# One exponential per unit of four heads over the compressed keys, rope tables on DVE, and a new issue order on every engine

## The chip, the cores and the metric

The kernel runs on one NeuronCore of a Trainium2 chip. The core has five instruction queues that run side by side and wait for one another only through semaphores: PE multiplies matrices (its weight loads are listed as PEld), ACT (ScalarE), DVE (VectorE) and POOL (GpSimd) work on tiles in SBUF and PSUM, and SP issues most DMAs. The metric is the device time of one execution in microseconds (us); less is better.

## What is computed

One decoder layer for 256 tokens of 1024 channels, all in float32. Cut to what matters here:

```python
h = rmsnorm(x, norm1_g); proj = h @ w_in                 # (256, 6308), split into the parts below
q_a = rope(rmsnorm(q_a)); k_s, k_w likewise              # 12 heads in 3 groups of 4, head width 64
kc = rope(rmsnorm(mlp(blocks of k_c))); vc = mlp(blocks of v_c)      # 15 compressed keys per group
s_cmp = q_a . kc * scale
p_cmp = softmax(where(c_end <= t, s_cmp, -1e30)) * mask  # 256 tokens x 15 keys, for each head
o_cmp = p_cmp @ vc
...                                                      # o_slc over chosen blocks, o_win over a window
y_a = gate0 * o_cmp + gate1 * o_slc + gate2 * o_win
y_b = dilated attention over (q_b, k_b, v_b)             # 12 heads in 3 groups
mixed = sigmoid(g_ma) * (y_a @ w_o_a) + sigmoid(g_mb) * (y_b @ w_o_b)
x = x + mixed @ w_out
out = x + square(relu(rmsnorm(x, norm2_g) @ w_up)) @ w_down
```

With 256 tokens all four selected blocks are always chosen, so the selected attention and the window attention are both plain causal attention here.

## The kernel before

**Products.** Every float32 matrix is split into two parts that PE multiplies fast: `hi` is a rounded copy and `lo` the rest, and a product is made of three matmuls (hi by hi, lo by hi, hi by lo). Weights come from HBM in 192 or so pieces of 128 x 768 (`raw`). For each piece ACT casts it to `wh` (line 345) and DVE subtracts to get `wl` (line 350); then PE uses it for 12 to 18 matmuls of 256 or 384 columns. The input x is scaled and split in the same way: ACT makes `hT0` (line 415), DVE makes `hT1` (line 416), from the four quarters `xg0` to `xg3` that SP loads.

**Stages.** First the projections for the compressed, selected and window keys and values, then the queries together with the small MLPs that make the compressed keys; then attention runs piece by piece between further projections (the dilated q, k, v and the gates); then the output projections, `w_out`, and the feed-forward layer, from about 275 us on, which is matmuls and weight splits and little else.

**A unit of attention** (`nsa(g, t)`) is one group of four heads and 128 tokens; there are six. For each head PE makes the scores in PSUM, DVE takes the negative maximum `nm` (line 791), and ACT computes `exp(score + nm)` into `P` for three segments: selected keys, window keys and the 16 columns of the compressed keys (line 781, `expo`). Each of these asks for the row sum (`accum_out`), for which ACT runs a second small instruction. DVE then takes reciprocals of the sums and multiplies them with the gates (lines 826 and 827), and `P` is scaled by them: on ACT for seven pairs of heads out of twelve (line 832), on DVE for four and on POOL for one (lines 836 and 838). PE transposes P, and ACT and DVE split it again (`phi`, `plo`).

**Rope tables.** Five tables `ropeg` (128 x 256) are the cosines and sines times a gain; POOL multiplies them in the opening (line 444).

**The order of the work.** Python generators write the program, and at the end `issue_order` fixes, for each engine, in which order its instructions stand: the table `ORDER` lists for each engine the numbers of the instructions as they were written. An engine takes its instructions strictly in that order. The residual input `x1` (1 MB) is loaded by SP at line 1101; the program's tiles share SBUF where their lives don't overlap, and a load into shared space has to wait for the last use of what was there.

Of the kernel before, what the change touches and what calls it, by code (L numbers as in the profile page):

```python
# [19 lines left out]
S = 256  # L20
# [14 lines left out]
     "vkb": 3, "vqb": 3, "pscale": "aaaaaavvavgv", "dbufs": 4, "cahead": 2, "oc": (), "seq": "gQKVqkvgggg", "vneed": "nsa5", "late": 999, "mbufs": 8, "mahead": 7, "cseg": "000000", "yact": "", "kvact": 0, "tab": "g", "b32": "v", "epsact": 0, "mlast": 1, "dchain": "dils0", "dneed": "nsa5", "dPb": 8, "dP": "P", "q2": 4, "l0": 8, "l1": 9, "l2": 7, "l3": 10, "hh": 3,  # L35
# [85 lines left out]
1 0 2 4 3 9+2 104 15 13 12 16 11 19 14 20 18 5 17 6 8 7 21+83 105+60 166 165 167+4 172 171 173+5 179 178  # L121
180+4 185 184 186+4 191 190 192+5 198 197 199+2""",
    "ACT": """
# [122 lines left out]
def hybrid_layer(ctx: ExitStack, tc: tile.TileContext, A, out):  # L246
# [802 lines left out]
    pump(proj(420, post_kv(2)))  # L1049
    od.add(make_rb())  # L1050
    st_["qa"] = [once([128, 6, S], F32R, f"qa{i}") for i in range(2)]
    st_["y"] = once([128, 8, S], F32, "y")

    def zipped(i):

# [231 lines left out]
```

## Time and profile before

| | |
|---|---|
| median of 3 runs | 459.05 us (459.05 to 459.7) |
| the profiled execution | 458.8 us |
| its span, from the first to the last instruction | 457.0 us |
| mean granted TensorE clock | 0.993 |

The profile is of one execution. The span leaves out 1.8 us that lie around it in the execution's own time. Where the text speaks of a clock, 1.0 is 2.4 GHz and 0.5 is 1.2 GHz. Times of instructions are counted from the start of the span.

### The profile page before, as it was taken

To read this page: it belongs to the slowest core of one execution; us is meant where nothing else is said; L and a number is where in the kernel's file an instruction comes from. 1 tells how busy PE (TensorE), PEld (TensorE's weight loads), DVE (VectorE), ACT (ScalarE), POOL (GpSimd) and SP (SyncE) were. 2 spreads that over 40 slices of the span, in tenths; PEclk is the share of its full clock that TensorE was granted. 3 is DMA by queue.
4 is the path that set the end of the run, shared out by engine and by line. 5 is a ranking of instruction groups with operands and counts; after the bars stand their busy time and mean duration, and the time that the engine had idled before them with its cause. 6 is when DMAs were issued, how large, how long until landed. Compare 5 with 4: busy or idle time off the path is not lost.

```text
span 457.0 us, 9071 instructions
## 1 busy us (share of the span) xinstructions
PE 445.6 (98%) x3413; PEld 431.1 (94%) x3413; DVE 358.0 (78%) x654; ACT 284.2 (62%) x622; POOL 83.7 (18%) x92
## 2 busy tenths in 40 slices
PE   4999999999999999999999999999999999999996
PEld 4999899899999999898999999999999999999996
DVE  3989999999999998899999886886856654555440
ACT  4855677678999778876775555665665634433330
POOL 2712121313041000200000001796322300000000
PEclk9799999999999999999999999999999999999999
DMA  8974586725535522541521647666666667677620
GB/s 304 367 244 146 154 287 181 236 89 167 157 105 141 171 70 71 175 140 68 162 82 42 199 128 231 201 193 186 205 184 195 183 187 210 185 216 199 179 78 13
DMA packets 29484, 76.92 MB, mean 168 GB/s; under 512 B 3664, under 2 KB 5120, under 8 KB 29312
## 3 DMA queue, kind: packets, MB, share of 16 engines
q1 hardware_dynamic: 28864, 74.77, 54.7%
q10 hardware_dynamic: 576, 1.57, 1.0%
q8 instruction: 27, 0.44, 0.4%
q14 instruction: 17, 0.14, 0.1%
HBM read 75.28 MB, written 1.05 MB: 167 GB/s over the span
## 4 chain that ended last, share of the span: by engine, by line
PE 93%; DVE 2%; ACT 2%; DMA 2%; issue 0%; ACTq 0%
PE acc L983 19%; PE acc L985 19%; PE acc L984 19%; PE acc L480 6%; PE acc L481 6%; PE acc L479 6%; PE tp L709 3%; PE acc L468 2%; DMA raw<-in_kv_c 2%; PE sp L754 1%; PE pvo L721 1%; ACT wh L345 1%; PE pvo L723 1%; PE tp L552 1%; PE dsp L920 1%; PE hacc L615 1%
## 5 line engine op out<-in xcount | busy, mean ns | idle before, releaser
L350 DVE TENSOR_TENSOR wl<-raw,wh 128x768 fp32r<-128x768 f32 (+2 forms) x183 | 177.6, 979 | 61.7 <-ACT wh L345 57.2
L345 ACT CAST wh<-raw 128x768 fp32r<-128x768 f32 (+1 forms) x182 | 149.6, 833 | 102.1 <-PE acc L984 74.5
L983 PE MATMUL acc<-u,wh 128*128 128x256 f32 x256 | 71.6, 280 | 0.0
L984 PE MATMUL acc<-u,wh 128*128 128x256 f32 x256 | 71.6, 280 | 0.0
L985 PE MATMUL acc<-u,wl 128*128 128x256 f32 x256 | 71.5, 279 | 0.0
L984 PE MATMUL acc<-h,wh 128*128 128x256 f32 x256 | 69.0, 280 | 0.0
L983 PE MATMUL acc<-h,wh 128*128 128x256 f32 x256 | 69.0, 279 | 0.0
L985 PE MATMUL acc<-h,wl 128*128 128x256 f32 x256 | 66.1, 279 | 0.0
L480 PE MATMUL acc<-wl,hT 128*128 128x384 f32 (+1 forms) x164 | 55.1, 350 | 0.3 <-DVE wl L350 0.3
L479 PE MATMUL acc<-wh,hT 128*128 128x384 f32 (+1 forms) x164 | 54.7, 348 | 0.0
L481 PE MATMUL acc<-wh,hT 128*128 128x384 f32 (+1 forms) x164 | 54.6, 347 | 0.0
L1159 POOL TENSOR_TENSOR r<-r 128x256 f32<-128x256 f32 x32 | 27.7, 866 | 128.7 <-ACT r L1158 127.5
L985 PEld LDWEIGHTS acc<-u,wl 128*128 128x128 f32 x256 | 48.2, 188 | 0.0
L983 PEld LDWEIGHTS acc<-u,wh 128*128 128x128 f32 x256 | 48.1, 188 | 0.0
L984 PEld LDWEIGHTS acc<-u,wh 128*128 128x128 f32 x256 | 48.1, 188 | 0.0
L983 PEld LDWEIGHTS acc<-h,wh 128*128 128x128 f32 x256 | 47.6, 188 | 0.0
L984 PEld LDWEIGHTS acc<-h,wh 128*128 128x128 f32 x256 | 47.4, 188 | 0.0
L985 PEld LDWEIGHTS acc<-h,wl 128*128 128x128 f32 x256 | 45.8, 188 | 0.0
L502 POOL TENSOR_TENSOR st<-st,nhalf 128x6 f32<-128x6 f32 (+1 forms) x16 | 21.6, 1348 | 92.8 <-DVE st L501 65.7
L984 PE MATMUL acc<-hT,wh 128*128 128x256 f32 x128 | 36.1, 293 | 0.0
L985 PE MATMUL acc<-hT,wl 128*128 128x256 f32 x128 | 35.9, 293 | 0.0
L983 PE MATMUL acc<-hT,wh 128*128 128x256 f32 x128 | 35.1, 290 | 0.0
(212 smaller groups left out, 986.9 us busy)
## 6 DMA issues: line engine op xcount, KB each, us to landing
raw<-in_cells SPq DMA_DIRECT2D x128, 384.0 KB, 3.4
raw<-in_cw SPq DMA_DIRECT2D x10, 384.0 KB, 3.2
raw<-in_q_a SPq DMA_DIRECT2D x8, 384.0 KB, 3.8
raw<-in_q_b SPq DMA_DIRECT2D x8, 384.0 KB, 3.4
raw<-in_k_b SPq DMA_DIRECT2D x8, 384.0 KB, 3.2
raw<-in_v_b SPq DMA_DIRECT2D x8, 384.0 KB, 3.1
raw<-in_kv_w SPq DMA_DIRECT2D x4, 420.0 KB, 6.7
raw<-in_kv_c ACTq DMA_DIRECT2D x4, 384.0 KB, 7.0
```

Source lines behind the costliest of these rows:

```text
L345: nc.scalar.copy(hi[:, :m], src)
L350: nc.vector.tensor_sub(lo[:, :m], src, f(hi[:, :m]))
L468: nc.tensor.matmul(acc[t][:, :n], hT[h][:, k, t * 128:(t + 1) * 128], w[:, kk * n:(kk + 1) * n], start=h == 0 and k == 0 and w is hi, stop ...
L479: nc.tensor.matmul(o, hT[0][:, k, ts], hi[:, c], start=k == 0, stop=False)
L480: nc.tensor.matmul(o, hT[0][:, k, ts], lo[:, c], start=False, stop=False)
L481: nc.tensor.matmul(o, hT[1][:, k, ts], hi[:, c], start=False, stop=k == 7)
L502: nc.gpsimd.tensor_tensor(st[:, 1, :h], st[:, 0, :h], nhalf[:, :h], op=OP.pow)
L709: nc.tensor.transpose(pt[0:rows, i * 128:(i + 1) * 128], s, ident)
L983: nc.tensor.matmul(o, hi, a[0][k], start=start, stop=False)
L984: nc.tensor.matmul(o, hi, a[1][k], start=False, stop=False)
L985: nc.tensor.matmul(o, lo, a[0][k], start=False, stop=stop)
L1159: mul = nc.gpsimd.tensor_mul(r, r, r)
```

## The change

Three things in the code. In `D`, `cseg` goes from all zeros to all ones: in each of the six units the compressed keys are taken apart from the other two segments. DVE adds `nm` to the 16 columns of each head and puts the four heads side by side into one tile `cP` (128 x 64); one exponential on ACT then does all four; DVE sums, takes the reciprocals, multiplies with the gates and scales. The path was in the code already (`apart`) and was not taken. Second, `tab` goes from `g` to `v`: the five rope tables are multiplied by DVE. Third, `y` and `x1` are allocated in another way, by which `x1` comes to share space with tiles of the stages before it. With these goes a new `ORDER` for all five engines.

```diff
-     "pscale": "aaaaaavvavgv", ... "cseg": "000000", ... "tab": "g",
+     "pscale": "aaaaaavvavgv", ... "cseg": "111111", ... "tab": "v",
...
 ORDER = {
     "SP": """
-1 0 2 4 3 9+2 104 15 13 12 16 11 19 14 20 18 5 17 6 8 7 21+83 105+60 166 165 167+4 172 171 173+5 179 178
+0+2 3 2 14 9 4 11 10 8 15 13 16 18 12 19+2 5 17 6+2 21+80 104 101+3 105+60 166 165 167+4 172 171 173+5 179
...
-    st_["y"] = once([128, 8, S], F32, "y")
+    st_["y"] = big.pool.tile([128, 8, S], F32, name="y", tag="y", bufs=1)
...
-    x1 = big.tile([128, 8, S], F32, name="x1", tag="y", bufs=1)
+    x1 = big.pool.tile([128, 8, S], F32, name="x1", tag="y", bufs=1)
```

The code that `cseg` switches, as it stands in both kernels:

```python
        def expo_c(r, src):
            if apart:
                nc.vector.tensor_scalar(cP[:, r], src, nm[:, r, 0:1], None, op0=OP.add)
            else:
                expo(r, 0, src, PP[r // 2][:, r % 2, 512:528])
...
        if apart:
            nc.scalar.activation(cP, cP, AF.Exp)
            nc.vector.tensor_reduce(den[:, :, 0], cP, axis=AX.X, op=OP.add)
            nc.vector.reciprocal(den[:, :, 0], den[:, :, 0])
            nc.vector.tensor_mul(den[:, :, 0], den[:, :, 0], gates[:, t, g * 4:g * 4 + 4, 0])
            nc.vector.tensor_mul(cP, cP, den[:, :, 0:1].to_broadcast([128, 4, 16]))
```

What the new order does at the places that the prediction speaks of. Lines in the rows of the changed kernel are 15 lower than in the kernel before. First the opening on ACT, before the change, from the table load on; `wh_160`, `wh_215` and `wh_219` are the second, third and fourth weight piece, `sx` are squares for the norm:

```order
L345 ACT_TABLE_LOAD
L345 CAST wh_160<-raw_83 128x768
L426 ACTIVATE sx1_181<-xg1_77 128x512
L345 CAST wh_215<-raw_86 128x768
L426 ACTIVATE sx0_180<-xg0_76 128x512
L415 ACTIVATE hT0_137<-xg0_76 128x256 x2
L415 ACTIVATE hT0_137<-xg1_77,xg0_76 128x256 x2
L426 ACTIVATE sx2_182<-xg2_78 128x512
L415 ACTIVATE hT0_137<-xg2_78,xg0_76 128x256 x2
L345 CAST wh_219<-raw_89 128x768
```

And the same place in the changed kernel:

```order
L400 ACT_TABLE_LOAD
L400 ACTIVATE hT0_137<-xg0_76 128x256 x2
L411 ACTIVATE sx0_180<-xg0_76 128x512
L400 ACTIVATE hT0_137<-xg1_77,xg0_76 128x256 x2
L411 ACTIVATE sx1_181<-xg1_77 128x512
L330 CAST wh_160<-raw_83 128x768
L400 ACTIVATE hT0_137<-xg3_79,xg0_76 128x256
L411 ACTIVATE sx3_183<-xg3_79 128x512
L400 ACTIVATE hT0_137<-xg3_79,xg0_76 128x256
L330 CAST wh_215<-raw_86 128x768
L400 ACTIVATE hT0_137<-xg2_78,xg0_76 128x256 x2
L330 CAST wh_219<-raw_89 128x768
```

The first half of hT0 stood behind two weight casts and two squares and now stands first; `xg0`, which it reads, is now the first load on SP and was the second.

Second, SP's queue where `x1` stands. Before, in the opening:

```order
L315 DMA raw_102<-in_kv_w 128x840
L381 DMA gr_104<-in_gr 128x768
L1101 DMA x1_3396<-in_xg 128x2048
L393 DMA cw2_114<-in_cw2 128x256
L389 DMA rowm_110<-in_rowm 128x1
L386 DMA posT_108<-in_posT 128x32
L315 DMA raw_116<-in_kv_w 128x840
```

And in the changed kernel, among the weights of the output projections (`raw_3349` and `raw_3375` here are the pieces that were issued at 235.6 and 241.1 us):

```order
L300 DMA raw_3297<-in_cells 128x768
L300 DMA raw_3323<-in_cells 128x768
L1086 DMA x1_3413<-in_xg 128x2048
L300 DMA raw_3349<-in_cells 128x768
L300 DMA raw_3375<-in_cells 128x768
L300 DMA raw_3401<-in_cells 128x768
```

The megabyte leaves the opening; its wait there (for a matmul of the last block of the dilated attention) now holds back the pieces behind it.

Third, DVE in the middle of the first unit, in the changed kernel (`nm_976` and `cP_978` belong to the first unit, `nm_1109` to the second; the `wl` are weight splits for PE):

```order
L776 TENSOR_REDUCE nm_976<-sp_979 128x2
L776 TENSOR_REDUCE nm_976<-sp_979 128x1
L513 TENSOR_TENSOR vq_954<-t1_949,st_945 128x384
L620 SCALAR_TENSOR_TENSOR z1_1021<-z1_1021,z0_1020 128x96
L776 TENSOR_REDUCE nm_976<-sp_1008 128x2
L776 TENSOR_REDUCE nm_976<-sp_1008 128x1
L776 TENSOR_REDUCE nm_1109<-sp_1137 128x1
L771 TENSOR_SCALAR cP_978<-sp_979,nm_976 128x16
L776 TENSOR_REDUCE nm_1109<-sp_1137 128x1
L623 SCALAR_TENSOR_TENSOR hid_1027<-z1_1021,z0_1020 128x96
L335 TENSOR_TENSOR wl_1126<-raw_892,wh_1125 128x768
L335 TENSOR_TENSOR wl_1169<-raw_900,wh_1168 128x768
```

The `cP` row is one of the 24 new ones; they stand between the maxima and the weight splits. Over the whole order, the DVE instructions that are no weight splits and stand ahead of the 24th weight split go from 65 to 63, ahead of the 48th from 140 to 167, and ahead of the 64th from 211 to 255.

## Rows read from the trace of the kernel before

**Rows 1.** The page: busy us, share of the span and instructions of each engine.

```profile
PE 445.6 (98%) x3413; PEld 431.1 (94%) x3413; DVE 358.0 (78%) x654; ACT 284.2 (62%) x622; POOL 83.7 (18%) x92
```

**Rows 2.** Windows of the opening: length, busy us of each engine, clock, DMA share, GB/s.

```profile
0.00:25.00 25.00, 18.46 (x85) 17.79 (x86) 17.35 (x22) 14.83 (x23) 13.14 (x22) 0.86 0.93 338
...
7.10:11.10 4.00, 0.00 (x0) 0.00 (x0) 1.89 (x3) 3.16 (x6) 0.42 (x2) 0.89 1.04 411
11.10:17.00 5.90, 5.88 (x18) 5.54 (x19) 5.90 (x8) 5.90 (x12) 4.00 (x3) 0.50 1.03 387
```

**Rows 3.** Timeline of the opening: start, us, engine, line; idle before and its end.

```profile
5.01 0.63 DVE L349 CAST wh<-raw 128x384 fp32r<-128x384 f32 x2 [5.01 <-DMA raw<-in_kv_c]
6.98 0.19 POOL L440 COPY g<-xg 128x8 f32<-128x8 f32 x1 [4.58 <-DMA xg<-in_xg]
10.57 0.89 ACT L415 ACTIVATE hT<-xg 128x256 fp32r<-128x256 f32 x2
11.12 3.13 PE L468 MATMUL acc<-wh,hT 128*128 128x384 f32 x8 [4.09 <-ACT hT L415]
```

**Rows 4.** The chain that ended last, opening: start, us, what.

```profile
11.12 7.27 PE acc L468 x24
18.56 1.04 PE acc L468 x6
```

**Rows 5.** Timeline, DVE beside POOL; and the clean hT1-sized form, by line.

```profile
18.44 5.24 POOL L444 TENSOR_TENSOR ropeg<-rope,gr 128x256 f32<-128x256 f32 x5 [1.26 <-DMA rope<-in_rope]
18.86 2.73 DVE L416 SCALAR_TENSOR_TENSOR hT<-xg,xg,hT 128x256 fp32r<-128x256 f32 x3
21.52 1.57 DVE L350 TENSOR_TENSOR wl<-raw,wh 128x840 fp32r<-128x840 f32 x1
L1118 DVE SCALAR_TENSOR_TENSOR h<-x,g,h 128x256 fp32r<-128x256 f32 x8 | 3.8, 482 | 0.2
```

**Rows 6.** Windows of the attention, columns as in rows 2.

```profile
91.00:150.00 59.00, 59.00 (x373) 54.92 (x372) 57.17 (x132) 52.55 (x165) 12.39 (x11) 1.00 0.47 135
150.00:205.00 55.00, 55.00 (x440) 51.11 (x438) 49.64 (x107) 42.94 (x120) 2.81 (x3) 1.00 0.41 119
```

**Rows 7.** The chain again, where PE last waited for a weight split.

```profile
50.87 0.95 DVE wl L350
51.87 0.44 PE acc L480
```

**Rows 8.** Groups by line and form, 85 to 215 us: count, busy us, mean ns.

```profile
L781 ACT ACTIVATION_READ_ACCUMULATOR P<-sp,nm 128x1 f32 x60 | 12.2, 203 | 0.0
...
L781 ACT ACTIVATE P<-sp,nm 128x16 f32<-128x16 f32 x24 | 6.5, 274 | 0.0
...
L832 ACT ACTIVATE P<-P,den 128x16 f32<-128x16 f32 x14 | 4.3, 304 | 0.0
...
L791 DVE TENSOR_REDUCE nm<-sp 128x1 f32<-128x16 f32 x24 | 3.8, 164 | 0.0
```

**Rows 9.** Timeline of DVE, small instructions back to back.

```profile
103.55 0.23 DVE L501 TENSOR_SCALAR st<-st,e 128x6 f32<-128x6 f32 x1
103.69 0.17 DVE L791 TENSOR_REDUCE nm<-sp 128x1 f32<-128x16 f32 x1
103.78 0.54 DVE L497 TENSOR_REDUCE st<-sq 128x6 f32<-128x384 f32 x1
```

**Rows 10.** Around x1: its landing, later weight loads, a matmul, a cast, x1's use.

```profile
x<-in_xg SPq DMA_DIRECT2D x1, 1024.0 KB, 8.9
235.58 14.66 SPq L315 DMA_DIRECT2D raw<-in_cells  x3
243.08 0.28 PE L721 MATMUL dpo<-phi,dv 128*128 128x128 f32 x1
253.96 0.84 ACT L345 CAST wh<-raw 128x768 fp32r<-128x768 f32 x1
L1116 DVE TENSOR_TENSOR x<-acc,x x8: 424/425/426, 262.9 to 274.0; 128x256 f32<-128x256 f32 x8
```

More of the change, by code (lines that the diff above doesn't have):

```diff
@@ L34 @@
      "xm": 4, "xn": 3, "rbufs": 5, "wbufs": 5, "xb": 3, "phib": 3, "Pb": 5, "sqb": 2, "t2b": 2, "t1b": 2,
-     "vkb": 3, "vqb": 3, "pscale": "aaaaaavvavgv", "dbufs": 4, "cahead": 2, "oc": (), "seq": "gQKVqkvgggg", "vneed": "nsa5", "late": 999, "mbufs": 8, "mahead": 7, "cseg": "000000", "yact": "", "kvact": 0, "tab": "g", "b32": "v", "epsact": 0, "mlast": 1, "dchain": "dils0", "dneed": "nsa5", "dPb": 8, "dP": "P", "q2": 4, "l0": 8, "l1": 9, "l2": 7, "l3": 10, "hh": 3,
+     "vkb": 3, "vqb": 3, "pscale": "aaaaaavvavgv", "dbufs": 4, "cahead": 2, "oc": (), "seq": "gQKVqkvgggg", "vneed": "nsa5", "late": 999, "mbufs": 8, "mahead": 7, "cseg": "111111", "yact": "", "kvact": 0, "tab": "v", "b32": "v", "epsact": 0, "mlast": 1, "dchain": "dils0", "dneed": "nsa5", "dPb": 8, "dP": "P", "q2": 4, "l0": 8, "l1": 9, "l2": 7, "l3": 10, "hh": 3,
      "hp_post": 100, "hp_cmp": 100, "hp_nsa": 0, "hp_dil": 100, "nb_acc": 4, "nb_oth": 6, "acc6": 4}
@@ L120 @@
     "SP": """
-1 0 2 4 3 9+2 104 15 13 12 16 11 19 14 20 18 5 17 6 8 7 21+83 105+60 166 165 167+4 172 171 173+5 179 178
-180+4 185 184 186+4 191 190 192+5 198 197 199+2""",
+0+2 3 2 14 9 4 11 10 8 15 13 16 18 12 19+2 5 17 6+2 21+80 104 101+3 105+60 166 165 167+4 172 171 173+5 179
+178 180+4 185 184 186+4 191 190 192+5 198 197 199+2""",
     "ACT": """
[15 rows of a table removed]
-474 473 475+3 479 478 481 480 482 484 483 485+3 489 488 491 490 492 494 493 495+3 499 498 501 500 502+38""",
-    "DVE": """
[20 rows of a table removed]
-635+2 634 637+4 643 641 644 642 645+4 650+2 649 652+2""",
-    "PE": """
[60 rows of a table removed]
-2575+17 2597 2592+3 2598 2595 2599+20 2620 2619 2621+767""",
[14 rows of a table added]
+440 442 441 443+3 447 446 449 448 450 452 451 453+3 457 456 459 458 460 462 461 463+3 467 466 469 468 470+38""",
+    "DVE": """
[21 rows of a table added]
+669 672+4 677+2 676 679+4 684+2 683 686+4 692 690 693 691 694+4 699+2 698 701+2""",
+    "PE": """
[46 rows of a table added]
+1861+9 1890+3 1870+2 1893+3 1899+7 1872 1896 1906+6 1873+2 1897+2 1912+1476""",
     "POOL": """
-28 25 2 15 14 0+2 7 3+3 11+2 10 9 8 6 13 18 17 16 19+3 23+2 22 26+2 34+2 38 37 40 29 39 30 33 31 36 32 42 41
-45+5 44 50+5 56 55 57+4 62 61 63+11 43 74+14""",
+1 23 2 20 9+2 0 7 3 8 4+3 11 13+2 12 15+2 18 17 19 22 21 29 28 24 31+2 34 25 33 27 26 30 35+11 47 46 48+34""",
 }
```

176 rows, old and new, of the table ORDER are left out of this document.

## The prediction

> **What bounds the kernel now.** I read the page first. PE is busy for 445.6 of 457.0 us [rows 1], so there are few us that an order could win, and the question is which. The windows show where they lie: from 7.1 to 11.1 us PE does nothing, and from 11.1 to 17.0 its granted clock is 0.50, half of the full 2.4 GHz [rows 2]. The timeline says what PE waited for there: the first half of hT0, which ACT began at 10.57 and which reads `xg0` [rows 3]. That quarter had landed by 6.98, when POOL's copy of it ran [rows 3]; hT0 stood behind casts and squares in ACT's queue. After that PE hardly stops, and the chain runs along PE nearly all the time. But it does not run alone. In the attention from 91 to 150 us DVE is busy for 57.17 of 59.00 us and ACT for 52.55; from 150 to 205 us DVE for 49.64 of 55.00 [rows 6]. The reader should see two engines that fill the same stretch: PE is the bound, DVE is 1.8 us short of being one. At 50.87 us the chain itself passes through a weight split on DVE and then the matmul that needed it [rows 7]. So an early start of PE is worth only as much as DVE can follow.
>
> **The opening: what PE can win.** In the changed order hT0 waits for `xg0` and the table load alone, and `xg0` is the first load of its queue. When it lands is bounded by 5.0 us, when the first weight piece had landed, and 6.98 us, when it had as second in the queue [rows 3]; I take 5.5, as the loads of one time land close together. Two halves of hT0 take ACT 0.89 us [rows 3], DVE makes two hT1 of 0.48 us clean [rows 5] and only then casts the first piece, in two halves of 0.32 us each [rows 3]: 5.5 + 0.45 + 0.96 + 0.32 = 7.2 us for the first matmul, against 11.12. That is 3.9 us, and 2.4 us if xg0 comes at 6.98. Then there is the clock. 24 matmuls from 11.12 on took 7.27 us, and six just after took 1.04 us, 0.173 each [rows 4]; 18 of the 24 are the window at 0.50 [rows 2], so these took (7.27 - 6 x 0.173) / 18 = 0.346 and lost 18 x 0.173 = 3.1 us. The clock fell while PE stood still and came back after some us of matmuls. If matmuls follow the warm-up without that pause, the fall need not happen. Against it stands the third piece: it needs the last of the four quarters of x, and ACT works through 8 halves of hT0 at 0.45 us, three casts and four squares to get there; the first two pieces are 24 matmuls, 4.2 us, so PE is there at 11.4 and I give 0.8 us for a wait (0 to 2). Together PE gains 3.9 + 3.1 - 0.8 = 6.2 us by about 17 us; 1.5 with the late landing, a fallen clock and a wait of 0.9.
>
> By the Trainium skill, page "TensorE: Matmul & The Clock Gate", Part 1 (What's actually happening), the throttled clock is the default and activity releases it. The trace agrees as far as it goes: 0.50 came after four idle us. No row here shows a start without that pause; by the page it would stay at full clock, and by the rows alone the 3.1 us could also stay lost, which is why (d) below has a chance.
>
> **The tables on DVE.** Five multiplications of 128 x 256 leave POOL (5.24 us) and come to DVE [rows 5]. The nearest DVE row of this size is 0.48 us, the dearest bound is POOL's own 1.05 us each [rows 5]: 2.4 us, 5.2 at most. But while POOL ran them, three hT1 on DVE took 0.91 us each instead of 0.48, and a split of 840 columns 1.57 us instead of 0.95 x 840 / 768 = 1.04 [rows 5, 7]: 1.29 + 0.53 = 1.8 us that DVE gets back. Net 0.6 us on DVE, from -0.6 (if the steps are shorter than the durations and overlap) to 3.4. It lies in the opening, where DVE idled 25.00 - 17.35 = 7.65 us [rows 2]. DVE's first instruction comes later there (it waits for hT0, at 5.95 instead of 5.01), but most of its later gaps go: 7.1 to 11.1 alone had 2.11 us [rows 2]. I count 1.5 us won. So DVE leaves the opening about 1 us ahead of before.
>
> **One exponential for four heads.** ACT loses 24 exponentials of 0.274 us with a sum read of 0.203 each, and 14 scalings of 0.304 us [rows 8], and gets six of about 0.3: 11.4 + 4.3 - 1.8 = 13.9 us less on ACT in the attention. DVE gets 24 additions of 128 x 16 from PSUM and 6 x 4 instructions for sum, reciprocal, gates and scaling, and loses four of the old scalings: 44 more. As durations, the nearest row is the maximum over 16 columns, 164 ns [rows 8], so 7.2 us; but small ones step faster than they last, the next one began 0.09 to 0.14 us later [rows 9], so 44 x 0.11 = 4.9 us. I take 4.9, range 4.0 to 7.2. What could hide it is DVE's idle time in the same stretch, 1.83 us from 91 to 150 and 5.36 us from 150 to 205 [rows 6]. Four of the six units' share, 3.3 us, falls before 150 by the order, so it does not fit there whole; I count half of the 1.83 as usable, because the rest is waits of some tenths for PE. DVE thus loses 2.4 us before 150, and nothing after, where 5.36 covers 1.6.
>
> By the Trainium skill, page "VectorE: DVE Perf Modes" (Specifications), VectorE sits closer to SBUF and ScalarE closer to PSUM, which speaks against giving DVE the reads from PSUM. The rows differ: 164 ns on DVE against 274 + 203 on ACT.
>
> **The order.** It moves more than the new instructions. Ahead of the 24th weight split DVE has two instructions fewer, although five tables are among them; the chain's split at 50.87 us lies near that place. So seven of the old ones have moved behind it; at 0.35 us each, an estimate between the 164 ns of a small one [rows 8] and the mean of 358.0 / 654 = 0.55 [rows 1], a split there comes 2.5 us earlier. Ahead of the 48th stand 27 more and ahead of the 64th 44 more: attention work has been pulled forward, and weights come later behind it.
>
> **x1.** Its 1 MB took 8.9 us to land in the opening, where the DMAs were full [rows 2, 10]. At 411 GB/s it is 2.5 us of them; PE waits for ACT there, so I count nothing for it beyond the times above. Now it is held until the last block of the dilated attention, whose matmul ran at 243.08 us [rows 10]. Two of the three weight loads that SP issued between 235.58 and 250.2 [rows 10] wait behind it. Issued at 243.5, and if they too take 8.9 us, they land at 252.4, ahead of the cast at 253.96; x1 is wanted at 262.9 [rows 10]. So nothing; without this cover, with a DVE that finishes the attention late, each us more than 1.5 is a us of PE.
>
> **The sum.** PE could lead by 6.2 us at 17 us. At about 50 us DVE allows 1 + 2.5 = 3.5 and what PE had waited there, about 1: 4.5. Less 2.4 until 150 us: 2.1. The rest of the program is the same on PE. The profiled execution of 458.8 becomes 456.7; the median stands 0.25 above it, so **456.9 us**.
>
> **Rivals.**
> (a) DVE follows the whole lead, because less waiting on ACT (13.9 us less work there) closes its gaps: 459.05 - 6.2 = 452.9. For it: 52.55 of 59.00 us of ACT in the same window [rows 6]. Against: DVE itself has more to do.
> (b) The lead is won and given back before 150 us, with DVE's lead used up by the instructions pulled forward: 459.05 +- 0.9. For it: 57.17 of 59.00 us [rows 6]; against it: the windows after 150 us have room. It comes out so if the opening gives DVE nothing and only the order's 2.5 us is left.
> (c) Slower: DVE becomes the bound in the attention. Its place is the splits behind the extra work, 48th to 64th; its price is 44 additions at their full durations, 7.2 us, less the 1.83 us of idle time and less a lead of 2.5: 2.9 us, 461.9. It decides when DVE's lead at 91 us is below what it must still take, 7.2 x 4/6 - 1.8 = 3.0 us.
> (d) The order does not bring PE forward, since x lands late and the clock falls as before: the lead is 1.5, DVE takes it, and the time is that of (b).
>
> **Chances.** Forecast, 454.5 to 458.1: 0.55. (a) 0.16. (b) and (d) 0.14. (c) 0.15. About 0.2%, 0.9 us, is what a measurement of this kernel can tell from no change. Faster is forecast and (a), 0.71; same 0.14; slower 0.15. The range goes from 452.8, which takes in (a)'s value, to 460.0, which leaves out most of (c).
>
> **What the profile after would show.** Right: PE's first real matmul at 7.0 to 8.8 us, no stretch of matmuls at 0.50 or one under 3.5 us; POOL without the five tables; hT1 at 0.5 us where POOL is idle; ACT's busy time 270 us; DVE's 362 or so; between 91 and 150 us DVE at 58 us or more of 59. The lead against before, read at the same matmul, is near 6 at 17 us and shrinks on waits of PE for `wl` and `plo`. Wrong: PE waiting for DVE by 3 us or more between 91 and 205, which is (c); or SP's load of x1 issued so late that casts near 254 us wait for DMA.

## The result, and the profile after

The changed kernel takes 456.82 us (median of four runs, 456.25 to 457.19), the kernel before on the same chip 459.05. The ratio is 0.9947, with a 95% interval from 0.9930 to 0.9965: 2.2 us faster, more than can be mistaken for no change. The forecast was 456.9. The profiled execution took 456.25 us with a span of 454.5, so the two spans differ by 2.5 us.

The page of the changed kernel, busy time by engine, answers [rows 1]:

```profile
PE 446.2 (98%) x3410; PEld 430.5 (95%) x3413; DVE 360.0 (79%) x703; ACT 275.7 (61%) x566; POOL 80.0 (18%) x86
```

ACT has lost 8.5 us, DVE has gained 2.0 for 49 more instructions, and PE has the same work in a shorter span (its count of 3410 lacks three records of the trace).

Windows of the changed kernel, columns as in [rows 2], for the opening, the stretch behind it, the attention, and 150 us of the feed-forward layer:

```profile
0.00:25.00 25.00, 21.37 (x115) 19.60 (x116) 18.78 (x31) 16.68 (x28) 9.88 (x17) 1.00 0.88 317
7.10:11.10 4.00, 3.75 (x20) 3.16 (x20) 4.00 (x6) 4.00 (x9) 1.52 (x1) 1.00 1.04 403
11.10:17.00 5.90, 5.88 (x34) 5.41 (x33) 5.29 (x9) 4.11 (x7) 2.74 (x2) 1.00 1.00 352
25.00:60.00 35.00, 34.63 (x219) 33.23 (x218) 34.70 (x72) 22.80 (x45) 5.94 (x5) 1.00 0.70 213
91.00:150.00 59.00, 58.96 (x376) 54.51 (x375) 58.22 (x140) 45.05 (x111) 10.11 (x9) 1.00 0.49 141
150.00:205.00 55.00, 54.68 (x429) 50.64 (x428) 52.28 (x127) 40.18 (x99) 4.74 (x4) 1.00 0.43 123
300.00:450.00 150.00, 150.00 (x1275) 149.95 (x1275) 83.94 (x107) 69.53 (x112) 26.01 (x29) 1.00 0.63 173
```

The four empty us of PE are gone, and the stretch behind them runs at a clock of 1.00 instead of 0.50: 34 matmuls where 18 were. In the attention DVE is busy for 58.22 of 59.00 us, 1.05 more than before, and ACT for 7.5 us less. From 25 to 60 us DVE has 0.3 us of idle time left.

Timeline of the changed kernel's opening (start, us, engine, line; idle before and what ended it), with SP's load of x1 at the end:

```profile
5.04 0.91 ACT L400 ACTIVATE hT<-xg 128x256 fp32r<-128x256 f32 x2 [0.71 <-DMA xg<-in_xg]
...
5.58 0.88 DVE L401 SCALAR_TENSOR_TENSOR hT<-xg,hT 128x256 fp32r<-128x256 f32 x2 [5.58 <-ACT hT L400]
...
6.88 1.65 PE L453 MATMUL acc<-wh,hT 128*128 128x384 f32 x8 [1.54 <-DVE wh L334]
...
14.26 2.23 POOL L432 TENSOR_TENSOR ropeg<-ropec,gr 48x128 f32<-48x128 f32 x1 [4.71 <-DMA gr<-in_gr]
...
16.45 3.32 POOL L413 TENSOR_TENSOR sx<-sx,sx 128x512 f32<-128x512 f32 x2
...
18.56 1.49 DVE L429 TENSOR_TENSOR ropeg<-rope,gr 128x256 f32<-128x256 f32 x1
...
19.82 0.83 PE L417 MATMUL tp<-ones,sx 128*128 128x1 f32 x6 [0.82 <-POOL sx L413]
...
19.97 1.02 DVE L335 TENSOR_TENSOR wl<-raw,wh 128x840 fp32r<-128x840 f32 x1
20.92 0.41 DVE L429 TENSOR_TENSOR ropeg<-rope,gr 128x256 f32<-128x256 f32 x1
...
23.34 1.82 DVE L335 TENSOR_TENSOR wl<-raw,wh 128x768 fp32r<-128x768 f32 x2
...
239.64 0.33 SPq L1086 DMA_DIRECT2D x<-in_xg  x1
```

hT0 now starts as soon as its quarter of x is there [rows 3], and PE's first real matmul stands at 6.88 instead of 11.12. The same kind of table on DVE takes 0.41 us while POOL is idle (at 20.92) and 1.49 beside POOL's addition of squares, and PE then waits for that addition.

Groups by line and form of the changed kernel, 85 to 215 us, columns as in [rows 8]: the new additions and the new exponential.

```profile
L771 DVE TENSOR_SCALAR cP<-sp,nm 128x16 f32<-128x16 f32 x23 | 5.1, 223 | 0.1
...
L825 ACT ACTIVATE cP<-cP 128x64 f32<-128x64 f32 x6 | 1.5, 258 | 0.6 <-DVE cP L771 0.6
```

To see where a lead is kept, I read for each kernel when PE had done the same amount of work (columns of its matmuls, counted along the order of its program) and subtracted that time from the time of before. The first line is before's own time in us, the last column stands near the end; a plus is a lead. So what stands in a column happened in the other kernel earlier by the lead: work of 25 us stands at 18.2 us in the changed kernel. Each row is one profiled execution, and that one need not be the median of its kernel: it was 0.6 us faster in the changed kernel, 0.6 slower in `add_twice`, 0.9 in `no_warm` and 1.7 in `four_exp`. The names are those of the experiments below.

```
us of before      17    25    30    50    70    91   110   130   150   205   270   450
changed          6.8   6.8   4.5   4.5   5.2   4.9   5.1   4.3   3.8   3.3   3.7   2.5
shifted          5.3   6.1   4.3   4.3   5.0   4.7   4.9   4.1   3.5   3.1   3.4   2.2
no_tables        5.2   6.0   4.6   4.6   5.3   5.0   5.2   4.3   3.8   3.4   3.7   2.5
no_warm          4.3   4.9   3.8   3.1   3.8   3.5   3.7   2.8   2.3   1.7   2.0  -0.5
add_twice        4.1   4.8   3.6   3.6   4.3   3.8   2.6   1.0   0.1  -3.3  -3.0  -4.2
tab_pool         5.4   6.2   4.7   2.7   3.4   3.1   3.3   2.4   1.9   1.4   1.8   0.6
four_exp         6.5   6.5   1.4   1.5   2.3   2.1   0.9  -0.9  -3.9  -6.0  -5.8  -5.6
open_old         1.2  -0.5  -1.5  -1.8  -1.2  -1.4  -1.3  -2.1  -2.6  -3.1  -2.8  -5.3
open_new         5.4   6.3   4.5   3.3   3.4   3.4   3.5   3.5   3.5   3.5   3.4   3.7
long_prefix      6.6   6.6   4.4   3.9   4.7   3.3   3.3   3.3   3.3   3.2   3.2   3.3
open_new_exp     6.6   6.6   4.4   3.2   3.3   3.3   3.4   1.3   0.9  -0.3  -0.6  -0.3
exp_old          0.0  -0.0  -0.0  -0.0  -0.0  -0.1  -0.1  -2.1  -2.5  -3.7  -4.0  -4.0
x1_late          0.9  -0.7  -0.7  -0.7  -0.7  -0.7  -0.6  -0.6  -0.6  -0.7  -0.8  -0.5
```

The changed kernel wins 6.8 us by 17, keeps 4.5 at 50, and gives back 1.4 between 110 and 150 and 0.5 to 205. It also loses 1.2 us in the feed-forward layer, where it has no instruction that before has not.

The fall from 6.8 to 4.5 lies between 18.2 and 25.5 us of the changed kernel. Part of it is PE's wait of 0.82 us for POOL's squares (at 19.82 above). The rest is not a wait: small matmuls stand there, of 1 and of 128 columns, which count for little work by this measure; some of them before has only from 30 us on. Behind this stretch the chain of the changed kernel, from 26 to 36 us, runs like this:

```profile
27.21 0.53 ACT kvT L568 x2
27.77 0.80 DVE wl L335
28.64 0.41 DVE vSW L548
29.09 0.63 DVE kvT L569 x2
29.73 0.88 DVE b L580
30.61 0.87 DVE wl L335
...
33.84 0.87 DVE wl L335
...
35.04 0.88 DVE blk L585
36.05 0.33 PE hacc L598
```

For eight us the chain runs through DVE, from one instruction to the next with gaps of under 0.2 us, and then PE takes over. DVE is the bound there, and the lead does not grow again before 50 us.

### The profile page after: what moved, and what is told of

It reads as the page before. It is cut to its first block, busy times and chain, and to the rows that moved or that the text cites. A ratio compares the mean times of both kernels' runs of the same rounds, so it can differ in the third digit from the quotient of the medians.

```text
span 454.5 us, 9070 instructions
## 1 busy us (share of the span) xinstructions
PE 446.2 (98%) x3410; PEld 430.5 (95%) x3413; DVE 360.0 (79%) x703; ACT 275.7 (61%) x566; POOL 80.0 (18%) x86
## 3 DMA queue, kind: packets, MB, share of 16 engines
HBM read 75.28 MB, written 1.05 MB: 168 GB/s over the span
## 4 chain that ended last, share of the span: by engine, by line
PE 91%; DVE 4%; DMA 3%; POOL 1%; issue 0%; ACT 0%; SPq 0%; POOLq 0%
PE acc L968 20%; PE acc L969 20%; PE acc L970 20%; PE acc L466 6%; PE acc L465 6%; PE acc L464 5%; PE tp L694 3%; DMA xg<-in_xg 1%; DMA gr<-in_gr 1%; PE sp L739 1%; PE dsp L905 1%; PE tp L537 1%; DVE wl L335 1%; PE pvo L708 1%; PE pvo L706 1%; PE hacc L600 1%
## 5 line engine op out<-in xcount | busy, mean ns | idle before, releaser
L970 PE MATMUL acc<-h,wl 128*128 128x256 f32 x256 | 71.6, 280 | 0.0
L969 PE MATMUL acc<-h,wh 128*128 128x256 f32 x256 | 71.6, 280 | 0.0
L968 PE MATMUL acc<-h,wh 128*128 128x256 f32 x256 | 71.5, 281 | 0.0
L465 PE MATMUL acc<-wl,hT 128*128 128x384 f32 (+1 forms) x164 | 56.1, 350 | 0.0
L464 PE MATMUL acc<-wh,hT 128*128 128x384 f32 (+1 forms) x164 | 55.5, 347 | 0.0
L466 PE MATMUL acc<-wh,hT 128*128 128x384 f32 (+1 forms) x164 | 55.2, 346 | 0.0
L1144 POOL TENSOR_TENSOR r<-r 128x256 f32<-128x256 f32 x32 | 30.6, 959 | 133.4 <-ACT r L1143 131.8
L969 PEld LDWEIGHTS acc<-h,wh 128*128 128x128 f32 x256 | 48.2, 188 | 0.0
L970 PEld LDWEIGHTS acc<-h,wl 128*128 128x128 f32 x256 | 48.2, 188 | 0.0
L968 PEld LDWEIGHTS acc<-h,wh 128*128 128x128 f32 x256 | 48.0, 188 | 0.0
L487 POOL TENSOR_TENSOR st<-st,nhalf 128x6 f32<-128x6 f32 (+1 forms) x16 | 23.0, 1443 | 104.2 <-DVE st L486 67.8
```

The lines of the kernel that those rows point to most:

```text
L464: nc.tensor.matmul(o, hT[0][:, k, ts], hi[:, c], start=k == 0, stop=False)
L465: nc.tensor.matmul(o, hT[0][:, k, ts], lo[:, c], start=False, stop=False)
L466: nc.tensor.matmul(o, hT[1][:, k, ts], hi[:, c], start=False, stop=k == 7)
L487: nc.gpsimd.tensor_tensor(st[:, 1, :h], st[:, 0, :h], nhalf[:, :h], op=OP.pow)
L968: nc.tensor.matmul(o, hi, a[0][k], start=start, stop=False)
L969: nc.tensor.matmul(o, hi, a[1][k], start=False, stop=False)
```

## The experiments

The ratios in the table are to the kernel before, measured beside it on the same chip, with their 95% intervals. "New" and "old" say whose opening (to 25 us, in `open_old` to 29) and whose attention order (behind it) a kernel has, and how many exponentials a unit has over the compressed keys.

| kernel | opening | attention | exponentials | median us | ratio to before |
|---|---|---|---|---|---|
| changed | new | new | 1 | 456.82 | 0.9947 (0.9930 to 0.9965) |
| open_new | new | old | 4 | 455.45 | 0.9933 (0.9920 to 0.9945) |
| open_old | old | new | 1 | 464.26 | 1.0115 (1.0102 to 1.0128) |
| exp_old | old | old | 1 | 462.83 | 1.0088 (1.0076 to 1.0100) |
| open_new_exp | new | old | 1 | 459.36 | 1.0010 (1.0001 to 1.0019) |
| four_exp | new | new | 4 in five units | 462.89 | 1.0092 (1.0074 to 1.0110) |
| long_prefix | new, to 76 us | old from 76 us | 4 | 455.64 | 0.9919 (0.9906 to 0.9933) |
| x1_late | old, x1 late | old | 4 | 459.82 | 1.0014 (1.0005 to 1.0023) |
| tab_pool | new, tables on POOL | new | 1 | 458.11 | 0.9976 (0.9967 to 0.9985) |
| no_tables | new, no tables | new | 1 | 456.28 | 0.9938 (0.9925 to 0.9952) |
| no_warm | new, no warm-up | new | 1 | 458.45 | 0.9991 (0.9982 to 1.0000) |
| add_twice | new | new, 24 more additions | 1 | 462.38 | 1.0074 (1.0062 to 1.0087) |
| shifted | new | new | 1 | 456.49 | 0.9946 (0.9934 to 0.9958) |

**The opening alone.** In `D` only the tables move; `ORDER` begins with the changed kernel's rows and goes on with those of before.

```diff
-     ... "cseg": "000000", ... "tab": "g",
+     ... "cseg": "000000", ... "tab": "v",
     "ACT": """
-0+4 6 10 13 9 4+2 7+2 11 16 15 14 17 12 19+2 25+4 18 21 47 22 24 35
+0+6 9 7+2 10 6 20 12 19 13 15+2 14 11 25 17 26+3 18 23+2 21+2 29 35
...
```

> The kernel before, with the changed opening alone: the first 25 us of the new order on ACT, DVE, PE and POOL, the new order of SP (x1 late too) and the five tables on DVE; from there on the old order and four exponentials. By the forecast's steps PE leads by about 6 us at 17 us, DVE lets 2 of them through (its 1 us and the 1 us that PE had waited; the 2.5 us of the reordered splits are not there), and nothing is taken back in the attention: 457.0, from 456.4 to 457.6. Rival, DVE follows the whole lead: 453. Rival, the lead is worth nothing without the new attention: 459.

It is faster by 0.67%, 3.1 us: more than the 2 that I let DVE pass on, and more than the whole change by its median, though the two intervals overlap. Its windows:

```profile
25.00:60.00 35.00, 33.35 (x206) 31.47 (x205) 33.82 (x71) 21.23 (x42) 5.29 (x5) 1.00 0.61 184
91.00:150.00 59.00, 59.00 (x379) 54.49 (x377) 57.23 (x130) 51.74 (x162) 12.40 (x11) 1.00 0.47 142
```

And PE's wait for a weight split, from PE's waits by line:

```profile
PE acc L477 <- DVE wl L347: 1.4, 2, 1.2
```

The longer of the two stands at 42.44 us. By it PE falls back from a lead of 4.5 at 30 us to 3.3 by 50 us and then keeps 3.5 to the end, through an attention in which DVE is as busy as before. So the old attention carries a lead through whole; what the opening is worth is settled before 50 us. The two rivals fall: neither is the whole lead followed, nor is it lost without the new attention.

**The rest alone.** The changed kernel with before's opening:

```diff
-     ... "tab": "v",
+     ... "tab": "g",
     "ACT": """
-0+6 9 7+2 10 6 20 12 19 13 15+2 14 11 25 17 26+3 18 23+2 21+2 29 35
+0+4 6 10 13 9 4+2 7+2 11 16 15 14 17 12 19+2 25+4 18 21 47 22+3 29 35
...
```

> The changed kernel with the opening of before: the first 29 us of the old order on every engine, the tables on POOL again, and x1 late as in the changed kernel; the new attention and its one exponential stay. By the forecast's steps the clock falls to 0.50 again, PE has no lead at 17 us, the new attention brings DVE 2.5 us at 50 us of which PE can use its 1 us of waiting, and then costs 2.4: 460.2, from 459.5 to 461. Rival, the new attention is itself where the gain comes from: 457.5 or less.

It is slower by 1.15%, 5.3 us, worse than I expected by 4. The table of leads splits this: it is 1.5 us behind at 30, as the kernel with only x1 moved is 0.7 behind; 1.6 more go from there to 205 us; 2.5 go in the feed-forward layer. The new attention is no gain by itself. The two halves do not add up: 3.1 won and 5.3 lost would make 2.2 us slower, and the changed kernel is 2.2 faster. By the leads, 1.5 us of this difference lies before 30 us, where `open_old` has x1 late beside the tables on POOL, 1.4 in the attention and 1.2 in the feed-forward layer.

**One exponential in the old order.** Only `cseg` changes; the new DVE and ACT rows stand where the old exponentials and scalings were.

```diff
-     ... "cseg": "000000", ... "tab": "g",
+     ... "cseg": "111111", ... "tab": "g",
```

> The kernel before with one exponential for four heads and nothing else: the new DVE and ACT instructions stand where the old exponentials and scalings stood, all else in the old order. By the forecast DVE pays 4.9 us for them, 3.3 of it before 150 us where it can hide half of 1.8: 2.4 us on PE, 461.4, from 460.4 to 462.4. Rival, ACT's 13.9 us less is worth as much to DVE's waits as the instructions cost: 459.0 or less.

It costs 0.88%, 4.0 us, where I had 2.4. The first unit is free (no loss at 110 us), 2.0 us go between 110 and 130, 2.0 later. The chain of this kernel at that place, and PE's row behind it:

```profile
122.19 0.86 DVE vk L522
123.06 0.16 DVE cP L784
...
123.23 0.27 ACT cP L838
...
123.52 0.23 DVE den L839
```

```profile
123.35 0.30 PE L707 MATMUL tp<-ident,P 128*128 128x128 f32 x1 [0.64 <-DVE cP L784]
```

The last of the four additions stands behind other work on DVE, and PE waits 0.64 us until it is done; only then can the exponential, the sum, the reciprocal and the scaling follow one another. How much of the 4.0 us this chain costs PE is not shown. What the trace does show is DVE's time: counted from the start of each to the start of the next instruction, the 48 new ones take 8.7 us here, 1.1 of it idle, and 6.7 in the changed kernel, 0.3 idle. From a sum to the next instruction there are 0.25 us here, where the reciprocal that needs it comes next, and 0.13 in the changed kernel, where in most units other work stands between (medians).

**One exponential with the new opening.** The same insertion into `open_new`:

```diff
-     ... "cseg": "000000", ... "tab": "v",
+     ... "cseg": "111111", ... "tab": "v",
```

> The changed kernel's opening with the old attention order, and one exponential in all six units: the same instructions as in the changed kernel, with only the order behind 25 us being the old one. If one exponential costs what it cost without the lead, 4.0 us, this is 459.4, from 458.6 to 460.2, and the new order of the attention is worth 2.6 us to the changed kernel. Rival, a lead of PE's weights covers it: 456 to 457.

Measured 459.36. Against `open_new` it costs 0.77% by the difference of the ratios, 3.5 us, with or without a lead: DVE's stretch gives nothing back. (SP's stores of the result near the end stand one place later here, which the diff doesn't show.) Against the changed kernel, which has the same instructions, it is 2.9 us slower: that much the new order behind the opening is worth. By the leads it is 3.6 at 205 us, 1.3 of it won by 50, and the changed kernel's feed-forward layer takes some back.

**Four exponentials in the new order.**

```diff
-     ... "cseg": "111111",
+     ... "cseg": "000100",
```

> The changed kernel, with its opening and its order, but with four exponentials again in five of the six units (the fourth keeps one exponential, for the space of the tiles): the 20 additions and the sums leave DVE there, and each exponential and scaling of 16 columns is back on ACT, right beside where the addition and the other scalings stand. If the small DVE instructions are what the attention costs the changed kernel (it loses about 2 us of its lead between 100 and 220 us), these come back: 454.0 to 455.5. Rival, the new order lives from ACT's 13.9 us less and PE now waits for ACT: 457 or more. Rival, the order and not the instructions is what takes the 2 us: 456.8 within 0.5.

It is 6.7 us slower than the changed kernel, on the side of the rival, and my theory of this run falls. The profiled execution took 464.58 us, 1.7 above this kernel's median and 8.3 above the profiled changed kernel. Of these 8.3, 3.1 (a lead of 1.4 instead of 4.5 at 30 us) come from the opening, where every engine has the same rows as in the changed kernel. `long_prefix` has these rows too and leads by 4.4 there, so the 3.1 us are not the price of four exponentials. The timeline of this kernel:

```profile
13.76 4.28 POOL L430 TENSOR_TENSOR ropeg<-ropec,gr 48x128 f32<-48x128 f32 x1 [3.94 <-DMA gr<-in_gr]
...
17.67 2.52 DVE L333 TENSOR_TENSOR wl<-raw,wh 128x840 fp32r<-128x840 f32 x1
...
21.36 0.83 PE L415 MATMUL tp<-ones,sx 128*128 128x1 f32 x6 [2.08 <-POOL sx L411]
```

And its windows:

```profile
23.00:25.00 2.00, 2.00 (x8) 1.88 (x7) 2.00 (x8) 1.25 (x3) 0.72 (x1) 0.57 0.14 53
...
91.00:150.00 59.00, 55.56 (x334) 49.75 (x332) 51.74 (x112) 46.73 (x140) 11.82 (x9) 1.00 0.48 143
```

POOL's small table took 4.28 us instead of 2.23, PE waited 2.08 instead of 0.82, and soon after the clock fell to half for about three us. The other part, from 2.3 at 70 us to -6.0 at 205, is the attention. There PE is idle for 3.4 of 59 us and DVE too has idle time; the longest wait of PE is this one, of PE's waits by line:

```profile
PE tp L692 <- ACT P L815: 2.0, 1, 2.0
```

PE waits for a scaling on ACT. So the new order, with these rows placed so, has no room for the work that was taken off ACT. How much of it another placing of these ACT rows would save was not tried.

**The new order for longer.** The changed kernel's rows to 76 us, then before's:

```diff
-     ... "cseg": "111111", ... "tab": "v",
+     ... "cseg": "000000", ... "tab": "v",
```

> The changed kernel's order up to 76 us on ACT, DVE, PE and POOL (and all of SP's), with the tables on DVE; from there on the old order, with four exponentials in every unit. The changed kernel leads by about 5 us there, the kernel with only the new opening by 3.4, and the latter kept all of it through the old attention. If the old attention keeps any lead that it is given, this is faster than both kernels: 453.8 to 454.8. Rival, the new order before 76 us only pays ahead what the old order then lacks (work that it has pushed behind), and the lead falls to 3.4 or less: 455.4 or more.

Measured 455.64, a ratio of 0.9919: the rival was right. The lead is 4.7 at 70 us and 3.3 at 91. PE's row at the seam:

```profile
80.86 0.33 PE L532 MATMUL tp<-ident,vq 128*128 128x128 f32 x1 [1.05 <-DVE vq L524]
```

The extra lead of the new order at 50 to 76 us is gone where the orders meet: PE waits for DVE work that the new order had put off. A cost of the seam itself would look the same, and this run does not tell the two apart. By its ratio this is the fastest kernel of the case: its interval lies just clear of that of `shifted` (0.9934 to 0.9958), which has the changed kernel's instructions and order; from the changed kernel's own and from that of `open_new` it is not clear.

**x1 alone.**

```diff
-1 0 2 4 3 9+2 104 15 13 12 16 11 19 14 20 18 5 17 6 8 7 21+83 105+60
+1 0 2 4 3 9+2 15 13 12 16 11 19 14 20 18 5 17 6 8 7 21+80 104 101+3 105+60
...
-    st_["y"] = once([128, 8, S], F32, "y")
+    st_["y"] = big.pool.tile([128, 8, S], F32, name="y", tag="y", bufs=1)
...
-    x1 = big.tile([128, 8, S], F32, name="x1", tag="y", bufs=1)
+    x1 = big.pool.tile([128, 8, S], F32, name="x1", tag="y", bufs=1)
```

> The kernel before with only the load of x1 moved from the opening to its place in the changed kernel. By the forecast nothing: 459.0 within 0.5, as PE waits for ACT's queue there. Rival, the DMAs are what is short in the opening and 2.5 us of them come free: 457 to 458.

It is slower by 0.14% (0.05 to 0.23), 0.6 us: not quite nothing, and not the rival's gain. The timeline of this kernel says why:

```profile
15.76 1.29 POOL L425 TENSOR_TENSOR sx<-sx,sx 128x512 f32<-128x512 f32 x1 [1.23 <-ACT sx L423]
15.77 1.56 DVE L413 SCALAR_TENSOR_TENSOR hT<-xg,xg,hT 128x256 fp32r<-128x256 f32 x1
...
23.86 0.64 PE L477 MATMUL acc<-wl,hT 128*128 128x420 f32 x2 [0.43 <-DVE wl L347]
```

And the first two of these in the kernel before:

```profile
15.55 0.47 DVE L416 SCALAR_TENSOR_TENSOR hT<-xg,xg,hT 128x256 fp32r<-128x256 f32 x1
...
15.71 1.46 POOL L428 TENSOR_TENSOR sx<-sx,sx 128x512 f32<-128x512 f32 x1 [1.23 <-ACT sx L426]
```

Before, this hT1 on DVE starts 0.16 us ahead of POOL's squares and takes 0.47 us; here it starts 0.01 us behind them and takes 1.56. That is 1.1 us lost on DVE, and PE then waits for it, 0.43 us in the row shown. POOL's tables start earlier too, at 17.01 instead of 18.44, but the splits and hT1 beside them take no longer than before. `open_old`, with the same rows of the opening, has the short hT1 and loses 0.5 us on the splits behind it; so where the two engines collide is a matter of some tenths of a us. The windows of `x1_late` show something else:

```profile
11.00:13.00 2.00, 1.84 (x5) 1.50 (x6) 2.00 (x4) 2.00 (x6) 1.33 (x2) 1.00 1.09 367
...
15.00:17.00 2.00, 2.00 (x13) 2.00 (x12) 2.00 (x2) 2.00 (x5) 1.25 (x1) 1.00 1.01 378
```

PE pauses as long as before, but 13 matmuls run from 15 to 17 us, where before 18 took the 5.90 us from 11.10: the slow stretch is shorter, after the same pause. (The 1.00 of the clock from 11 to 13 us is no reading: the first clock record of this trace begins at 14.79 us, and a stretch without a record counts as 1.00.) It led by 0.9 us at 17 and had lost it by 25.

**Tables on POOL.** Behind the power of the norm on POOL:

```diff
-     ... "tab": "v",
+     ... "tab": "g",
     "POOL": """
-1 23 2 20 9+2 0 7 3 8 4+3 11 13+2 12 15+2 18 17 19 22 21 29 28
+1 28 2 25 14+2 0 7 3 13 4+3 11+2 10 9 8 16 18+2 17 20+2 23 22
...
```

> The changed kernel with the five tables back on POOL, behind its power of the norm; all else in the new order. By the forecast's price (DVE loses 2.4 us to the tables and gets 1.8 back because POOL is out of its way) PE hardly moves: 456.8 within 0.6. Rival, the tables on DVE are dear and taking them away brings 1 to 2 us: 455 to 456. Rival, POOL beside DVE costs more than the tables: 458 or more.

The second rival came true: 1.3 us slower than the changed kernel, with the tables at this place on POOL. The timeline of `tab_pool`:

```profile
21.87 5.21 POOL L428 TENSOR_TENSOR ropeg<-rope,gr 128x256 f32<-128x256 f32 x5
...
23.57 2.92 DVE L334 TENSOR_TENSOR wl<-raw,wh 128x768 fp32r<-128x768 f32 x2
```

The same two splits took 1.82 us in the changed kernel (its timeline above, at 23.34). They lose 1.1 us beside POOL, and the lead at 50 us is 2.7 instead of 4.5.

**No tables.** This kernel leaves out the gains in the five tables.

```diff
-            tab = const.tile([128, NT, 2, 64], F32, name=f"ropeg{kind}")
-            eng = nc.vector if D["tab"] == "v" else nc.gpsimd
-            eng.tensor_mul(tab, rope, gr[:, :, kind][:, None].to_broadcast([128, NT, 2, 64]))
-            ropeg[kind] = tab
+            ropeg[kind] = rope
```

> The changed kernel without the five multiplications of the tables: the rope tables are used without their gains, which is left out. DVE has five instructions of 0.41 us less in the opening. If DVE sets PE's pace from 17 us on, PE gains 1 to 2 us: 455 to 456. Rival, PE's pace there is set by ACT, POOL's squares or the weights: 456.8 within 0.4.

Measured 456.28, 0.4 us less than the changed kernel by the difference of the ratios, which is within what the two intervals leave open: the tables on DVE cost next to nothing, so in the opening DVE does not set PE's pace alone.

**No warm-up.**

```diff
-    warm = acc_bank()
-    for i in range(D["warm"]):
-        nc.tensor.matmul(warm[:, 0:128], ones, ones, start=True, stop=True)
```

> The changed kernel without the ten warm-up matmuls. If the clock stays up because matmuls follow the warm-up without a long pause, then without it the first matmuls run at 0.50 and PE has lost about 3 us by 17 us, of which the end sees what DVE had let through: 458 to 459. Rival, the first real matmuls bring the clock up quickly or the lead is cut by DVE anyway: 456.8 within 0.5.

2.0 us slower than the changed kernel. Its first real matmuls, in the timeline:

```profile
7.00 2.26 PE L448 MATMUL acc<-wh,hT 128*128 128x384 f32 x6 [7.00 <-DVE wh L332]
```

Six take 2.26 us, where eight took 1.65 in the changed kernel. It is 2.5 us behind the changed kernel at 17 and 1.4 at 50 to 91; the rest, 1.3 us, is lost in the feed-forward layer, at a full clock and for a reason that no run shows. So that the time fell into the forecast's range is partly luck. Nor does this run show that the warm-up brings the clock up: `add_twice` has the warm-up, and its first 24 matmuls are as slow (7.00 us, 7.04 here).

**Each addition twice.**

```diff
                 nc.vector.tensor_scalar(cP[:, r], src, nm[:, r, 0:1], None, op0=OP.add)
+                nc.vector.tensor_scalar(cP[:, r], src, nm[:, r, 0:1], None, op0=OP.add)
```

> The changed kernel with each of the 24 additions of 128 x 16 written twice in a row (the second does the same again), so 24 more small DVE instructions in the attention. If DVE sets the pace there, as the forecast has it, they cost 24 x 0.11 = 2.6 us of DVE, two thirds of it before 150 us with under 1 us to hide it: 458.3 to 459.3. Rival, DVE has room: 456.8 within 0.4.

5.8 us slower than the changed kernel. The rows of the tile `cP` in this kernel, with least, median and greatest duration in ns:

```profile
L770 DVE TENSOR_SCALAR cP<-sp,nm x24: 203/226/234, 84.5 to 196.4; 128x16 f32<-128x16 f32 x24
L771 DVE TENSOR_SCALAR cP<-sp,nm x24: 232/234/236, 84.7 to 196.6; 128x16 f32<-128x16 f32 x24
```

From 70 to 205 us it loses 7.6 us of lead, the changed kernel 1.9: 5.7 us for 24 additions, 0.24 each. PE pays for nearly all of it; DVE has next to no room there. The price is twice what I had put. Part of that is the experiment's own: the second addition writes the same place and starts 0.26 us after the first, while the instruction behind a single one starts after 0.14 (medians in this trace and in the changed kernel's).

**Other places in SBUF.**

```diff
-    nhalf = const.tile([128, 16], F32, name="nhalf")
+    nhalf = const.tile([128, 768], F32, name="nhalf")
```

> The changed kernel with one constant tile of 16 columns made 768 wide (POOL fills it, the rest is not read), which shifts the other tiles' places in SBUF by 3 KB and leaves every instruction and order as it was. The step from one matmul to the next in the feed-forward layer was 117.3 ns before and 117.7 to 118.8 in kernels with other places, always at a clock of 1.0. If it hangs on the places, it changes here, by 0.3 ns or more over 1536 matmuls, and the time with it by 0.5 us or more. Rival, it hangs on the order of the instructions: 117.7 and 456.8 within 0.4.

Nothing moves: 456.49, and as many matmuls in the same 150 us. The theory of the places falls, as far as a shift of 3 KB can test it. The rival, the order of the instructions, is not borne out by the other runs either: in the new order `four_exp` has 1285 matmuls in these 150 us and `no_warm` 1265. The windows of before, of `shifted`, and of `no_warm`:

```profile
300.00:450.00 150.00, 150.00 (x1282) 149.95 (x1281) 86.84 (x111) 72.16 (x117) 29.91 (x33) 1.00 0.62 179
```

```profile
300.00:450.00 150.00, 150.00 (x1275) 149.95 (x1275) 84.28 (x107) 69.89 (x112) 26.26 (x29) 1.00 0.62 173
```

```profile
300.00:450.00 150.00, 150.00 (x1265) 149.95 (x1264) 85.34 (x108) 70.97 (x115) 27.03 (x31) 1.00 0.63 175
```

## Why the prediction was right, and where it was not

The picture held: an early start of PE, of which only a part is kept, and an attention that takes some of it back. That 456.9 met 456.82 to a tenth of a us is luck: terms that were off cancelled, and 1.2 us were lost in a part that the sum had at nothing.

**The start.** "7.2 us for the first matmul" came at 6.88, since `xg0` landed by 5.04 and not at 5.5. The lead of 6.2 by 17 us was 6.8. The third piece's wait for x did not come as such; PE waited in small pieces for the splits.

**The clock's 3.1 us** were in the sum for 17 us, and in the profiled execution they came: no slow matmul at all. But the reason that I gave, no long pause, is not what the runs show. The first 24 real matmuls took 7.11 us before, 6.03 in `x1_late` and 5.85 in `open_old` after the same pause; with the early start and a short pause they took 5.04 in the changed kernel, 5.82 in `open_new` and `shifted`, 7.00 in `add_twice`. What differs is when the granted clock rises. Nine kernels have the new opening and the warm-up; in five of their traces the clock record at full speed begins by 6.3 us (at 4.90 in the changed kernel; in `open_new` it rose at 4.28 and fell again from 7.69 to 11.11), in four not before 10.2 (at 10.44 in `shifted`, 13.23 in `add_twice`). So these 3.1 us came by the luck of one execution. And they are worth little at the end: `shifted`, with the changed kernel's instructions, is 1.5 us behind it at 17 and 0.2 at 30. PE's later waits cover a lost 1.5 us, for splits and for POOL's squares (0.35 us in `shifted` where the changed kernel waits 0.82); of the 2.5 to 2.7 that `no_warm` and `add_twice` lost, about 1 us stayed.

**"At about 50 us DVE allows 4.5"** was 4.5, by two terms that were mis-sized against each other. I had 1 from the opening, 2.5 from the order and 1 of PE's own waiting. The opening alone passes on 3.3 to 3.5 where I had 2, and the new order adds 1.2 at 50 us where I had 2.5; in `long_prefix` this part is gone again by 91 us. Nor is it DVE's splits that cut the lead from 6.8 to 4.5 in the changed kernel: PE's one wait there is for POOL's squares. Where the lead is cut by DVE is `open_new`, from 4.5 to 3.3 between 30 and 50 us.

**The tables.** "Net 0.6 us" of cost to DVE had the wrong sign: moved back to POOL they cost 1.3 us, left out they bring 0.4. The step that failed is the credit for POOL being out of the way: I counted it from three hT1 and one split, 1.8 us, and took the tables' own price from the clean row. By the Trainium skill, page "SBUF — State Buffer", section "SBUF: two separate sides", DVE and GpSimd share one pair of ports; a DVE instruction with two inputs from SBUF and a GpSimd one that reads SBUF exclude each other there, and whichever starts first holds the pair to its end while the other stands still. The trace agrees: a table waits on DVE for 1.49 us instead of 0.41 beside an addition on POOL, and a split of 840 columns for 2.52 instead of 1.02.

**One exponential, "DVE loses 2.4 us before 150, and nothing after"**: the sum was near and its place was not. In the changed kernel 5.1 of lead at 110 became 3.8 at 150 and 3.3 at 205, 1.8 us in all. But this is a difference of two larger terms that I had not seen apart: 3.5 to 4.0 us for the instructions in the old order, less what the new order gives back. The 4.9 us of DVE were under-priced by the step of 0.11 us: a single new addition steps by 0.14 us, and the 48 new instructions take 6.7 us of DVE in the changed kernel and 8.7 in the old order, less some 0.4 for the four old scalings. ACT's busy time fell by 8.5 us and not by 13.9, since its short rows overlap: in the trace of before an exponential of 16 columns and its sum read step by 0.156 and 0.093 us, where I had added 0.274 and 0.203. The 5.36 us of DVE's idle time after 150 us did not cover what I said they would: `exp_old` loses 1.5 us after 150 us, from -2.5 to -4.0.

**x1, "nothing"**: 0.6 us slower alone, in the trace by a collision of DVE and POOL. What x1 late is worth in the changed kernel, no run shows: none has it early there, as none has four exponentials in all six units in the new order. The megabyte was issued at 239.64 and landed in 4.7 us instead of 8.9 [rows 10], and was wanted at 258.7.

**"The rest of the program is the same on PE"** is the step that failed most plainly: 1.2 us were lost between 270 and 450 us, in 1275 matmuls for 150 us against 1282, at a full clock and with no wait. Without it the profiled gain would have been 3.7 us. Why the matmuls step more slowly stays open.

Of the rivals, (a) is refuted by the time, 456.82 against 452.9, and by the lead, which is 4.5 at 30 us and not 6.2. (b) did not happen: 3.8 of the lead is left at 150 us. Nor did (c): PE is idle for 0.4 us between 91 and 205 us. Without the new opening the kernel is slower indeed, by 5.3 us (`open_old`). (d) did not happen.

## What to carry to other kernels

Run the opening and the middle of a change that moves everything apart, and do not expect them to add up: here one half is worth 3.1 us, the other costs 5.3, and together they give 2.2. Where a second engine is busy for 57 of 59 us, price each new instruction on it at its full step and give it no cover; and let instructions that need one another's results stand apart in its queue, since the same 48 took 8.7 us of it in one order and 6.7 in the other. Give POOL its work where DVE is idle, not merely where POOL is idle itself. And read the spacing of the matmuls in the opening before you credit a change with a faster clock there: two executions of the same instructions differed by 1.5 us at 17 us.

## What the runs showed of the hardware that was not expected

**When the clock first rises differs from one execution to the next.** In `x1_late` the clock's column reads 1.00 from 11 us on, but eight of the first matmuls stood 0.32 us apart, the pace of before at 0.50, against 0.173 later. In `no_warm` 17 did. By the Trainium skill, page "TensorE: Matmul & The Clock Gate", Part 1, the trace's clock events are not wholly to be trusted; here the records that there are agree with the matmuls. The first one, at full clock, begins at 14.79 us in `x1_late` and at 13.09 in `no_warm`, just where the spacing changes, and so it does in `shifted` (10.44) and `add_twice` (13.23). Before its first record the trace tells nothing of the clock, and the column then reads 1.00; the spacing of the matmuls fills the gap. What decides between an early and a late rise is not settled by these runs.

**A matmul's step in the feed-forward layer is not one number.** At a clock of 1.00, without waits, 150 us held 1282 matmuls before, 1275 in the changed kernel and in `shifted`, and 1265 in `no_warm` and in `open_old`: 117.0, 117.6 and 118.6 ns each. Over the layer's 1536 matmuls that is 1 to 2.5 us. A shift of the tiles by 3 KB does not change it, and `no_warm` differs from the changed kernel by its warm-up matmuls alone. The cause stays open.

**A small table of 48 x 128 on POOL** took 0.72 us before, 2.23 in the changed kernel and 4.28 in `four_exp`, where DVE was busy beside it from end to end. POOL's squares start behind it, and PE waited for these, 0.82 us in the changed kernel and 2.08 in `four_exp`.
